# Eight of sixteen gate tiles as seven block products, with sums of the normed tokens kept in the residual's buffer

## Chip, cores and metric

One core of one Trainium2 chip runs the whole kernel in one launch. The metric is device time in microseconds (us), median of several runs. "Before" is the kernel as it stood, "after" the changed one.

## What is computed

One encoder layer on 1024 tokens of 1024 channels in float32. The part that matters here is the middle, where the normed tokens u meet one large input projection:

```python
u = rms_norm(h, mix_norm[i])
z = u @ w_in[i]
q, k, v, s_in, gates = jnp.split(z, splits, axis=-1)
y_attn = neighbourhood_attention(q..., k..., v..., na_rpb[i]) @ w_attn_out[i]
y_ssm = s5_branch(s_in, ...) @ w_ssm_out[i]
g_attn, g_ssm = jnp.split(jax.nn.sigmoid(gates), N_BRANCH, axis=-1)
h = h + (g_attn * y_attn + g_ssm * y_ssm) @ w_out[i]
```

In front of it and behind it stands a SwiGLU feed-forward block; a per-layer embedding and a last norm end the kernel. `gates` has 2048 columns: 16 tiles of 128 columns.

## The kernel before, in words

Everything lies transposed: channels on the 128 partitions, tokens along the free dimension, in two halves t = 0 and 1 of 512 tokens. A product in float32 accuracy is made by `mm3` of three matmuls on rounded parts (hi and lo of weight and tokens): hi times hi, hi times lo, lo times hi. `split` makes these parts: ScalarE casts hi, VectorE subtracts to get lo. One output tile of 128 columns for one half of the tokens (`proj`) takes 8 blocks of 128 channels, so 24 matmuls of 512 tokens.

The feed-forward blocks already run their large products in seven block products instead of eight (a 2 by 2 block scheme of the Strassen-Winograd kind). The names are in `A7` (which token operand: a block of the tokens, or one of the sums s1 to s4), `ACC7` (which of three PSUM banks X, Y, Z it adds to) and `NEW7`; `b_operand` makes the weight operand of product i from four raw weight blocks, in place, and splits it.

The middle part runs in this order on TensorE, and that order is the one in which the code is written. First `sin`, the four tiles of the state-space input, in two groups of two tiles, with two gate tiles (`gate_tile`, tile name gt) between; then `v`; then four rounds over head pairs (hp), each with the pair's q and k tiles (`qk_proj`) and 2, 2, 2 and 6 gate tiles; then the rest. A generator, `mixer_side`, is stepped by `tick()` once after every `mm3`. It sets between these matmuls, one after the other:

- the norm of the second token half (`u_second`), which writes the normed tokens to a scratch tile xn and splits them into u;
- 16 `inject` steps (8 small matmuls each: the state-space input of two groups, read back from memory, tile names ut and fmi) that fill the state buffer X, which uses the bytes of the residual's buffer h;
- the scan over X on GpSimd (`scan_steps`, 128 steps of three operations, each step needing the one before);
- 64 units of attention (8 heads, 2 row blocks, 4 column blocks). Unit j does the scores s of j, the transposes pt of unit j-3 and the products O of unit j-5. Between, VectorE adds the bias and takes the row maximum (sm), ScalarE takes the exponential, VectorE the reciprocal, ScalarE scales; pt is copied and split by ScalarE (pth) and VectorE (ptl). From unit 48 on each unit also starts one of 16 `ssm_out` steps: xs is copied out of X when the scan has ended, operands emi are loaded, and the products yo follow three units later;
- the state-space branch's gated linear unit (glu).

`yield n` in that generator means: go on after n ticks. A unit takes 4 ticks (12 large matmuls), and 3 from unit 48 on. A unit whose head pair has not been projected yet waits for it in the written order (`while hd not in qkv: yield 1`).

VectorE, ScalarE, GpSimd and the DMA queue of SyncE (SP) each have an order of their own here, made ahead of time by a planner that places an instruction when it expects its inputs and its buffer; at run time every engine and queue keeps that order and waits where it must. Buffers come from pools: 56 of 2 KB for each partition (tag x; u alone holds 32), 12 of 4 KB (tag w: split weights, q, k, xs), 3 of 4 KB (st: raw weights) and 4 (tmp).

Of the kernel before, what the change touches and what calls it, by code (L numbers as in the profile page):

```python
# [8 lines left out]
F32 = mybir.dt.float32  # L9
# [29 lines left out]
def encoder_block(ctx, tc, I, out):  # L39
# [22 lines left out]
    def tx(name, dt=F32R):  # L62
        return tl("x", NX, [P, HT], dt, name)
# [20 lines left out]
    def tmq(name, shape=(P, HT)):  # L84
        return at("tmp", shape, F32, name)
# [100 lines left out]
    def hsl(t):  # L186
        return slice(t * HT, (t + 1) * HT)
# [20 lines left out]
    class Norm:  # L208
# [37 lines left out]
            rstd(m, r, q)  # L246
            self.r = r

        def apply(self, gi, res, every):

            for j in range(NK):
                xn = tmq("xn")
                with behind_():
                    V.scalar_tensor_tensor(xn, self.h[j][self.t], gains[:, gi, j:j + 1], self.r, ALU.mult, ALU.mult)
                hi, lo = tx("xh"), tx("xl")
                split(hi, lo, xn)
                res.append((hi, lo))
                yield every
# [16 lines left out]
                    post(m)  # L275
            m0 += lead

    def halves(h, gi, store=None):


        xn = [[], []]
        nn = [Norm(h, 0), Norm(h, 1)]

        def done(m, t):
            nn[t].add(m)
            if store is not None:
                store(m, t)

        def first():
            yield 22  # L290
            nn[0].stat()
            yield 4
            yield from nn[0].apply(gi, xn[0], 5)

        def second(wait, every):
            yield wait
            nn[1].stat()
            yield every
            yield from nn[1].apply(gi, xn[1], every)

        return xn, done, first, second

# [17 lines left out]
    class Seven:  # L320
# [71 lines left out]
        def put(self, name, src):  # L392
            hi, lo = self.a21[len(self.ops[name])] if name == "a21" else (tx("xh"), tx("xl"))
            if self.plain:
                split(hi, lo, src)
                self.ops[name].append((hi, lo))
                return
            with behind_():
                self.last.append(split(hi, lo, src).ins)
            self.ops[name].append((hi, lo))  # L400
# [18 lines left out]
                    self.put(name, self.h[j0 + k][1])  # L419
                    yield 1  # L420

    def b_operand(blk, i):

        b11, b12, b21, b22 = blk
        if i in (2, 3, 6):
            V.tensor_tensor(b11, (b12, b22, None, None, b21)[i - 2], b11, ALU.subtract)  # L426
        elif i == 5:
            V.tensor_tensor(b12, b22, b12, ALU.subtract)
        hi, lo = tw("wh", [P, HT]), tw("wl", [P, HT])
        mark["ins"] = split(hi, lo, (b21, b11, b11, b11, b22, b12, b11)[i]).ins  # L430
        return hi, lo

# [563 lines left out]
    def store_h(m, t):  # L996
        nc.scalar.dma_start(h_d[:, (2 * m + t) * HT:(2 * m + t + 1) * HT], h[m][t])

    u, done, u_first, u_second = halves(h, 1, store_h)

    def t0_done():
        start(u_first())
# [36 lines left out]
    def proj(w, t, name):  # L1039
        o = bank(name)  # L1040
        for k in range(NK):
            mm3(o, w[k], u[t][k], k == 0, k == NK - 1)
            tick()
        return o


    X = tl("h", 1, [P, 2 * XR], F32, "X")
    Xt = X[:, 0:1]
# [4 lines left out]

    Xv = X.rearrange("p (r g n) -> p r g n", r=2, g=NPAIR)

    def load_u(pr):
        ut = thid("ut", [P, 2, NCH], F32)
        nc.sync.dma_start(ut, u_d[2 * pr:2 * pr + 2].rearrange("g p c -> p g c"))
        return ut

    def inject_load(pr):
        fm = thid("fmi", [P, HT], F32)
        nc.sync.dma_start(fm, f_d[pr])
        return load_u(pr), fm

    def inject(pr, ut, fm):
        o = bank("inj")
# [218 lines left out]
    stored = set()  # L1286

    def mixer_side():
        yield from u_second(14, 1)
        yield 8  # L1290
        for r in range(2):
            V.memset(Xv[:, r, :, 0:1], 0.0)
            V.memset(Xv[:, r, :, XP - 1:XP], 0.0)
        ld = {}
        for pr in range(NPAIR):
            if pr in (0, 8):
                while pr // 4 not in stored:
                    yield 1
                yield 8
                ld[pr] = inject_load(pr)  # L1300
                yield 8
# [67 lines left out]
    for m0 in range(0, 4, 2):  # L1369
        W = [(loadw if m0 else lambda src: loadh(src, "hid", "hid"))(win[12 + m0 + i]) for i in range(2)]  # L1370
        Wx = [loadw(win[16]), loadw(win[17])] if m0 == 0 else []
        su = [tst("su"), tst("su")]
        for t in range(2):
            for i in range(2):
                o = proj(W[i], t, "sin")
                A.copy(su[i].rearrange("p (s c) -> p c s", s=L)[:, t * 64:(t + 1) * 64, :],
                       o.rearrange("p (c s) -> p c s", s=L))
            for i, w in enumerate(Wx):
                gate_tile(w, i, t)
        for i in range(2):  # L1380
            for g in range(8):
                nc.sync.dma_start(u_d[8 * (m0 + i) + g].rearrange("(s i) c -> i s c", s=L),
                                  su[i][g * 16:(g + 1) * 16].rearrange("i (s c) -> i s c", s=L))
            stored.add(m0 + i)


    Wv = [loadw2(I["wv"][i]) for i in range(4)]
# [46 lines left out]
            res += [(hi[:, ksl(k)], lo[:, ksl(k)]) for k in range(4)]  # L1434
        return res

    gm = 2
    for hp in range(4):
        wq, wk = loadw(win[hp]), loadw(win[4 + hp])
        w = loadw(win[16 + gm])  # L1440
        qk_proj(hp, wq, wk)
        n = 2 if hp < 3 else 6
        for i in range(n):
            wn = loadw(win[17 + gm]) if i < n - 1 else None
            for t in range(2):
                gate_tile(w, gm, t)
            gm += 1
            w = wn
# [313 lines left out]
```

## Time and profile before

| what | us |
|---|---|
| runs | 2116.14, 2117.87, 2118.72; median 2117.87 |
| the profiled execution's own time | 2118.57 |
| its span, first to last instruction | 2116.8 |
| TensorE busy | 2089.2 (99%) |
| VectorE, ScalarE, GpSimd busy | 1416.2, 978.3, 387.3 |
| first `sin` matmul, first attention unit, last unit's scores | 685.2, 836.8, 1086.3 |

The page of the profile gives busy time, the span in 40 slices, the chain of work that ended last and the costliest groups. Views of the trace used below: the timeline (start, duration, instruction, and in brackets the idle time before it with what ended it), groups by line, windows (busy time of each engine in a stretch), and waits. A matmul's duration in it overlaps the next one's; what counts on TensorE is the distance from start to start.

### The profile page before, as it was taken

How to read it: one execution, taken by the hardware profiler on the slowest of the kernel's cores; microseconds unless marked ns; L12 is line 12 of the kernel's file. 1: busy time of each engine (PE TensorE's matmuls, PEld its weight loads, DVE VectorE, ACT ScalarE, POOL GpSimd, SP SyncE). 2: the span in 40 equal slices, each digit the busy share in tenths (PEclk: the TensorE clock that was granted, in tenths of full speed). 3: DMA queues.
4: the chain of work that ended last, by engine and by line, in shares of the span. 5: the costliest groups of instructions: out<-in, count | busy, mean ns of one | idle time of the engine just before them, and what ended most of it. 6: DMA issues, size and time to landing. Idle time of an engine off the chain costs nothing.

```text
span 2116.8 us, 28037 instructions
## 1 busy us (share of the span) xinstructions
PE 2089.2 (99%) x9708; PEld 1716.0 (81%) x9708; DVE 1416.2 (67%) x2416; ACT 978.3 (46%) x1793; POOL 387.3 (18%) x620
## 2 busy tenths in 40 slices
PE   8999999999999999999999999999999999999998
PEld 3788888888888888888888788788888888888886
DVE  7897776667967334777743666896565665785855
ACT  6434333334445344666764422553333334445544
POOL 0047555540000007888100000000000000000000
PEclk9999999999999999999999999999999999999999
DMA  3435444485543552223577631242423338533302
GB/s 132 142 117 153 128 130 131 138 282 157 183 120 106 157 179 67 82 82 96 150 200 260 209 105 52 93 155 95 129 80 120 100 100 290 171 107 95 116 24 80
DMA packets 195150, 280.98 MB, mean 133 GB/s; under 512 B 41280, under 2 KB 80320, under 8 KB 195008
## 3 DMA queue, kind: packets, MB, share of 16 engines
q1 hardware_dynamic: 180160, 258.22, 38.9%
q10 hardware_dynamic: 14848, 20.98, 2.9%
q8 instruction: 76, 1.25, 0.2%
q14 instruction: 66, 0.54, 0.1%
HBM read 196.81 MB, written 82.31 MB: 132 GB/s over the span
## 4 chain that ended last, share of the span: by engine, by line
PE 90%; DVE 5%; ACT 2%; DMA 1%; issue 1%; SPq 0%; DVEq 0%; ACTq 0%
PE dx L182 4%; PE dx L183 4%; PE dx L184 4%; PE ux L182 3%; PE gx L182 3%; PE ux L183 3%; PE ux L184 3%; PE gx L184 3%; PE gx L183 3%; PE gt L182 3%; PE gt L183 3%; PE gt L184 3%; PE dy L183 2%; PE dy L182 2%; PE dy L184 2%; PE uy L182 2%
## 5 line engine op out<-in xcount | busy, mean ns | idle before, releaser
L151 ACT CAST wh<-hbuf 128x512 fp32r<-128x512 f32 x280 | 172.9, 622 | 391.9 <-PE gx L183 81.9
L152 DVE TENSOR_TENSOR wl<-hbuf,wh 128x512 fp32r<-128x512 f32 x280 | 210.5, 754 | 124.3 <-ACT wh L151 122.0
L151 ACT CAST wh<-wblk 128x512 fp32r<-128x512 f32 x162 | 100.5, 623 | 166.9 <-PE dx L183 72.7
L152 DVE TENSOR_TENSOR wl<-wblk,wh 128x512 fp32r<-128x512 f32 x162 | 111.8, 692 | 46.6 <-ACT wh L151 41.2
L152 DVE TENSOR_TENSOR al<-araw,ah 128x512 fp32r<-128x512 f32 x154 | 106.4, 695 | 51.1 <-PE dx L183 21.1
L182 PE MATMUL dx<-ah,wh 128*128 128x512 f32 x352 | 137.9, 392 | 0.3 <-DVE hbuf L692 0.3
L1094 POOL TENSOR_TENSOR sc<-X,rho 128x128 f32<-128x128 f32 x128 | 78.1, 610 | 327.6 <-ACT X L1077 317.7
L184 PE MATMUL dx<-ah,wl 128*128 128x512 f32 x352 | 137.0, 389 | 0.0
L183 PE MATMUL dx<-al,wh 128*128 128x512 f32 x352 | 136.9, 389 | 0.0
L182 PE MATMUL gx<-xh,wh 128*128 128x512 f32 x320 | 124.9, 390 | 1.2 <-DVE c L579 1.2
L182 PE MATMUL ux<-xh,wh 128*128 128x512 f32 x320 | 125.1, 391 | 0.1
L184 PE MATMUL ux<-xh,wl 128*128 128x512 f32 x320 | 124.5, 389 | 0.0
L184 PE MATMUL gx<-xh,wl 128*128 128x512 f32 x320 | 124.5, 389 | 0.0
L183 PE MATMUL gx<-xl,wh 128*128 128x512 f32 x320 | 124.5, 389 | 0.0
L183 PE MATMUL ux<-xl,wh 128*128 128x512 f32 x320 | 124.5, 389 | 0.0
L151 ACT CAST ah<-araw 128x512 fp32r<-128x512 f32 x154 | 94.8, 619 | 45.6 <-PE dx L183 12.6
L182 PE MATMUL gt<-xh,wh 128*128 128x512 f32 x256 | 102.7, 401 | 0.0
L184 PE MATMUL gt<-xh,wl 128*128 128x512 f32 x256 | 99.8, 390 | 0.0
L183 PE MATMUL gt<-xl,wh 128*128 128x512 f32 x256 | 99.8, 390 | 0.0
L426 DVE TENSOR_TENSOR hbuf<-hbuf 128x512 f32<-128x512 f32 x120 | 91.3, 762 | 2.1
L182 PEld LDWEIGHTS dx<-ah,wh 128*128 128x128 f32 x352 | 66.1, 188 | 14.9 <-DVE hbuf L692 0.7
L183 PEld LDWEIGHTS dx<-al,wh 128*128 128x128 f32 x352 | 66.1, 188 | 13.9 <-issue 0.5
(376 smaller groups left out, 5719.8 us busy)
## 6 DMA issues: line engine op xcount, KB each, us to landing
araw<-a_d SPq DMA_DIRECT2D x154, 256.0 KB
a_d<-c SPq DMA_DIRECT2D x148, 256.0 KB
wblk<-in_wd SPq DMA_DIRECT2D x88, 256.0 KB
hbuf<-in_wg SPq DMA_DIRECT2D x40, 512.0 KB
hbuf<-in_wu SPq DMA_DIRECT2D x40, 512.0 KB
wst<-in_win SPq DMA_DIRECT2D x26, 512.0 KB
hbuf<-in_xT SPq DMA_DIRECT2D x32, 256.0 KB
h_d<-hbuf ACTq DMA_DIRECT2D x32, 256.0 KB
```

The source lines that it names most:

```text
L151: A.copy(hi, src)
L152: return eng.tensor_tensor(lo, src, hi.bitcast(F32), ALU.subtract)
L182: T.matmul(o, lhsT=wh, rhs=xh, start=first, stop=False, skip_group_check=more)
L183: T.matmul(o, lhsT=wh, rhs=xl, start=False, stop=False, skip_group_check=more)
L184: T.matmul(o, lhsT=wl, rhs=xh, start=False, stop=last, skip_group_check=more)
L426: V.tensor_tensor(b11, (b12, b22, None, None, b21)[i - 2], b11, ALU.subtract)
L1094: G.tensor_tensor(sc, both, rho4, ALU.mult)
```

## The change

Gate tiles 0 to 7 (of 16) are taken out of the places named above and computed in a stage of their own, between `sin` and `v`, in four groups of two tiles. Each group takes seven block products of 12 matmuls. For these, the token sums s1 to s4 are made by a new generator `u_sums`: the norm's `apply` with `keep` writes the normed tokens back into the residual's buffer h in place of xn, and the sums are made there, in place. The four `sin` tiles run first, all for t = 0 and then all for t = 1, with `u_second` and `u_sums` beside them. `mixer_side` starts only then; its inject steps now come every 6 ticks inside the gate stage, and their two loads share one buffer of the w pool (inj). The four rounds over head pairs keep 0, 1, 1 and 4 gate tiles; a unit of attention takes 2 or 3 ticks in turn, and 2 from unit 48 on.

```diff
-        def apply(self, gi, res, every):
+        def apply(self, gi, res, every, keep=False):
             for j in range(NK):
-                xn = tmq("xn")
+                xn = self.h[j][self.t] if keep else tmq("xn")
...
-    def b_operand(blk, i):
+    def b_operand(blk, i, packed=False):
...
-        hi, lo = tw("wh", [P, HT]), tw("wl", [P, HT])
+        if packed:
+            w = tw("wg")
+            hi, lo = w[:, 0:HT], w[:, HT:2 * HT]
+        else:
+            hi, lo = tw("wh", [P, HT]), tw("wl", [P, HT])
...
+    def u_sums(every):
+        a, b, c, d = ([h[j0 + k][t] for k in range(4)] for t in range(2) for j0 in (0, 4))
+        def put(name, src, lo=None):
+            hi, lo = tx("xh"), tx("xl") if lo is None else lo
+            split(hi, lo, src)
+            seven.setdefault(name, []).append((hi, lo))
+        for k in range(4):
+            V.tensor_tensor(d[k], c[k], d[k], ALU.add)
+            V.tensor_tensor(c[k], a[k], c[k], ALU.subtract)
+            put("s1", d[k])
+            yield every
+        for k in range(4):
+            V.tensor_tensor(a[k], d[k], a[k], ALU.subtract)
+            V.tensor_tensor(b[k], b[k], a[k], ALU.subtract)
+            put("s2", a[k])
+            yield every
+        while not sin_done:
+            yield 1
+        for name, src in (("s4", b), ("s3", c)):
+            for k in range(4):
+                if k % 2 == 0:
+                    two = tw("sl")
+                put(name, src[k], two[:, hsl(k % 2)])
+                yield every
+    seven = {"a12": u[0][4:], "a11": u[0][:4]}
+    start(chain(u_second(8, 1), u_sums(1)))
+    W = [loadh(win[12 + m], "hid", "hid") for m in range(2)] + [loadw(win[14 + m]) for m in range(2)]
+    su = [tw("su", dt=F32) for _ in range(4)]
...
+    for t in range(2):
+        for m in range(4):
+            o = proj(W[m], t, "sin")
+            A.copy(su[m]..., o...)
+            if t == 1:
+                for g in range(8):
+                    nc.sync.dma_start(u_d[8 * m + g]..., su[m][g * 16:(g + 1) * 16]...)
+            elif m > 1:
+                gate_raw(0, m - 2)
...
     def mixer_side():
-        yield from u_second(14, 1)
...
-            if pr in (0, 8):
-                while pr // 4 not in stored:
-                    yield 1
-                yield 8
-                ld[pr] = inject_load(pr)
-                yield 8
-            if pr % 8 < 7:
+            if pr == 0:
+                ld[0] = inject_load(0)
+                yield 4
+            if pr < NPAIR - 1:
                 ld[pr + 1] = inject_load(pr + 1)
             inject(pr, *ld.pop(pr))
-            yield 3
+            yield 6
...
-            yield 4 if j < SO else 3
+            yield 2 + (j % 2 if j < SO else 0)
...
+    def gate_seven(gp, i):
+        hi, lo = gops.pop((gp, i))
+        a, z = ACC7[i], gz.setdefault(gp, {})
+        if NEW7[i]:
+            z[a] = bank("g" + a.lower())
+        while len(seven.get(A7[i], ())) < 4:
+            force()
+        for k in range(4):
+            mm3(z[a], (hi[:, ksl(k)], lo[:, ksl(k)]), seven[A7[i]][k], NEW7[i] and k == 0, k == 3, not NEW7[i])
+            tick()
+        with tc.high_priority(offset=PRI):
+            c = (11, 11, 22, 12, 12, 22, 21)[i]
+            if i in (0, 2, 3, 6):
+                z[c] = tmp("gs")
+                A.copy(z[c], z[a])
+            else:
+                V.tensor_tensor(z[c], z[a], z[c], ALU.add)
+            if i in (1, 4, 5, 6):
+                gate_out(2 * gp + c % 10 - 1, c // 10 - 1, z[c])
...
+    for n, (gp, i) in enumerate(items):
+        if i in (0, 3):
+            gate_raw(gp + 1, i // 3)
+        gate_prep(*(items + [(4, 0)] * 3)[n + 3])
+        gate_seven(gp, i)
...
-    gm = 2
+    gm = 8
     for hp in range(4):
         wq, wk = loadw(win[hp]), loadw(win[4 + hp])
-        w = loadw(win[16 + gm])
+        n = (0, 1, 1, 4)[hp]
+        w = loadw(win[16 + gm]) if n else None
         qk_proj(hp, wq, wk)
-        n = 2 if hp < 3 else 6
```

TensorE has 9106 rows before and 9058 after. The first place to look at is the start of the gate work on TensorE. Before, a gate tile (gt) follows the second `sin` tile of the first half:

```order
L183 MATMUL sin_6207<-xl_6010,whh_6163 128x512
L184 MATMUL sin_6207<-xh_6009,whl_6164 128x512
L182 MATMUL gt_6253<-xh_5746,wh_6169 128x512
L183 MATMUL gt_6253<-xl_5747,wh_6169 128x512
L184 MATMUL gt_6253<-xh_5746,wl_6170 128x512
```

After, all `sin` tiles are done, the first product goes to bank Z (gz), the first inject step (inj) follows it, then the second product (bank X, gx):

```order
L183 MATMUL gz_6566<-xl_6002,wg_6550 128x512
L184 MATMUL gz_6566<-xh_6001,wg_6550 128x512
L1131 MATMUL inj_6582<-inj_6547 128x128 x4
L182 MATMUL gx_6596<-xh_5745,wg_6553 128x512
L183 MATMUL gx_6596<-xl_5746,wg_6553 128x512
```

So the first inject step stands 12 matmuls behind the last `sin` tile, and the next ones 18 matmuls apart. Their loads stand on the SP queue. Before, with the stores of the state-space input (u_d from su) in groups of 8 and the loads (fmi, ut) behind each:

```order
L1382 DMA u_d<-su 16x8x128 x8
L1058 DMA ut<-u_d 128x2x128
L1063 DMA fmi<-f_d 128x512
L1058 DMA ut<-u_d 128x2x128
L1382 DMA u_d<-su 16x8x128 x8
```

After, the load of the first step stands behind 16 of these stores, that of the second behind all 32:

```order
L1101 DMA u_d<-su 16x8x128 x16
L1123 DMA inj<-f_d 128x512
L1124 DMA inj<-u_d 128x2x128
L1101 DMA u_d<-su 16x8x128 x16
L1123 DMA inj<-f_d 128x512
L1124 DMA inj<-u_d 128x2x128
```

The second place is attention unit 48, the first that needs the last head pair. On TensorE before, its scores (s) stand 21 large matmuls behind the pair's last k matmul:

```order
L182 MATMUL gt<-xh,wh 128x512
L183 MATMUL gt<-xl,wh 128x512
L184 MATMUL gt<-xh,wl 128x512
L1209 MATMUL s<-kh,qs 128x288
L1210 MATMUL s<-kl,qs 128x288
```

After, three gate matmuls lie between the last k matmul and these scores:

```order
L183 MATMUL k<-xl,wh 128x512
L184 MATMUL k<-xh,wl 128x512
L182 MATMUL gt<-xh,wh 128x512
L183 MATMUL gt<-xl,wh 128x512
L184 MATMUL gt<-xh,wl 128x512
L1270 MATMUL s<-kh,qs 128x288
L1271 MATMUL s<-kl,qs 128x288
```

On VectorE, the rows between the maximum of unit 47 (sm) and that of unit 48 are, before:

```order
L1213 ISA sm,stat<-s,tb 128x288
L1213 ISA stat 128x1
L1113 COPY xs<-X 64x256 x4
L1229 TENSOR_TENSOR ptl<-pt,pth 96x384
L1195 TENSOR_TENSOR tb<-row,colm 128x12x24
L1160 SCALAR_TENSOR_TENSOR kl<-k,kh 64x512 x2
L1217 RECIPROCAL stat<-stat 128x1
```

and after, with a weight's split (wl), two pieces of the bias table (tb), three reciprocals and the copies xs ahead of the lo part kl of the keys:

```order
L1256 TENSOR_TENSOR tb<-row,colm 128x384
L1278 RECIPROCAL stat<-stat 128x1
L152 TENSOR_TENSOR wl<-wst,wh 128x1024
L1290 TENSOR_TENSOR ptl<-pt,pth 96x384
L1256 TENSOR_TENSOR tb<-row,colm 128x12x24
L1278 RECIPROCAL stat<-stat 128x1
L1174 COPY xs<-X 64x256 x2
L1278 RECIPROCAL stat<-stat 128x1
L1174 COPY xs<-X 64x256 x2
L1221 SCALAR_TENSOR_TENSOR kl<-k,kh 64x512 x2
```

The feed-forward blocks ahead of and behind the middle part keep their order, except that the first half's norm and splits, near the end of the first block, stand a few rows elsewhere on ScalarE and VectorE.

More of the change, by code (lines that the diff above doesn't have):

```diff
@@ L276, in down, with halves @@
             m0 += lead
-    def halves(h, gi, store=None):
+    def halves(h, gi, store=None, keep=False):
         xn = [[], []]
@@ L292, in first @@
             yield 4
-            yield from nn[0].apply(gi, xn[0], 5)
+            yield from nn[0].apply(gi, xn[0], 5, keep)
         def second(wait, every):
@@ L298, in second @@
             yield every
-            yield from nn[1].apply(gi, xn[1], every)
+            yield from nn[1].apply(gi, xn[1], every, keep)
         return xn, done, first, second
@@ L997, in store_h @@
         nc.scalar.dma_start(h_d[:, (2 * m + t) * HT:(2 * m + t + 1) * HT], h[m][t])
-    u, done, u_first, u_second = halves(h, 1, store_h)
+    u, done, u_first, u_second = halves(h, 1, store_h, True)
     def t0_done():
@@ L1044, in proj, with gate_raw @@
         return o
+    def u_sums(every):
[26 more added lines that the diff above has]
+    su = [tw("su", dt=F32) for _ in range(4)]
+    sin_done = []
+    gbl = {}
+    def gate_raw(gp, i):
+        if gp < 4:
+            st = tst("graw")
+            nc.sync.dma_start(st, win[16 + 2 * gp + i])
+            b = gbl.setdefault(gp, [None] * 4)
+            b[i], b[2 + i] = st[:, 0:HT], st[:, HT:2 * HT]
+    for t in range(2):
+        for m in range(4):
+            o = proj(W[m], t, "sin")
+            A.copy(su[m].rearrange("p (s c) -> p c s", s=L)[:, t * 64:(t + 1) * 64, :],
+                   o.rearrange("p (c s) -> p c s", s=L))
+            if t == 1:
+                for g in range(8):
+                    nc.sync.dma_start(u_d[8 * m + g].rearrange("(s i) c -> i s c", s=L),
+                                      su[m][g * 16:(g + 1) * 16].rearrange("i (s c) -> i s c", s=L))
+            elif m > 1:
+                gate_raw(0, m - 2)
+    seven["a22"] = u[1][4:]
+    sin_done.append(True)
+    drain()
     X = tl("h", 1, [P, 2 * XR], F32, "X")
@@ L1054, in encoder_block, with inject_load @@
     Xv = X.rearrange("p (r g n) -> p r g n", r=2, g=NPAIR)
-    def load_u(pr):
-        ut = thid("ut", [P, 2, NCH], F32)
+    def inject_load(pr):
+        both = tw("inj", dt=F32)
+        ut = both[:, HT:HT + 2 * NCH].rearrange("p (g c) -> p g c", g=2)
+        nc.sync.dma_start(both[:, 0:HT], f_d[pr])
         nc.sync.dma_start(ut, u_d[2 * pr:2 * pr + 2].rearrange("g p c -> p g c"))
[L1059 to L1064, printed above, removed]
+        return ut, both[:, 0:HT]
     def inject(pr, ut, fm):
@@ L1284, in glu_out @@
         nc.scalar.dma_start(y2_d[ksl(m), hsl(t)], sg)
-    stored = set()
     def mixer_side():
-        yield from u_second(14, 1)
-        yield 8
         for r in range(2):
@@ L1366, in gate_tile, with gate_prep, gate_out @@
         nc.sync.dma_start(g_d[m, :, hsl(t)], gs)
[L1369 to L1384, printed above, removed]
+    gops, gz = {}, {}
+    def gate_prep(gp, i):
+        if gp < 4:
+            gops[gp, i] = b_operand(gbl[gp], i, True)
+    def gate_out(m, t, z):
+        nc.sync.dma_start(g_d[m, :, hsl(t)], z)
+    def gate_seven(gp, i):
[17 more added lines that the diff above has]
+                gate_out(2 * gp + c % 10 - 1, c // 10 - 1, z[c])
+    items = [(gp, i) for gp in range(4) for i in range(7)]
+    for it in items[:3]:
+        gate_prep(*it)
+    for n, (gp, i) in enumerate(items):
[3 more added lines that the diff above has]
+        gate_seven(gp, i)
     Wv = [loadw2(I["wv"][i]) for i in range(4)]
```

1 line of the change is left out of this document (removed).

## The prediction

> **What bounds the kernel now.** First the page: busy time, GpSimd's line of the 40 slices, and the chain that ended last.
>
> ```profile
> PE 2089.2 (99%) x9708; PEld 1716.0 (81%) x9708; DVE 1416.2 (67%) x2416; ACT 978.3 (46%) x1793; POOL 387.3 (18%) x620
> POOL 0047555540000007888100000000000000000000
> PE 90%; DVE 5%; ACT 2%; DMA 1%; issue 1%; SPq 0%; DVEq 0%; ACTq 0%
> ```
>
> TensorE is the bound almost everywhere, so the next views are the waits of TensorE and the windows of the middle part: attention units 0 to 47, then unit 48 up to the first glu matmul.
>
> ```profile
> PE yo L1119 <- DVE ot L1244: 1.8, 1, 1.8
> PE v L1395 <- DVE wl L152: 0.6, 1, 0.6
> PE dn L182 <- ACT mh L151: 1.4, 1, 1.4
> ```
>
> ```profile
> 836.80:1019.80 183.00, 183.00 (x1066) 158.88 (x1065) 132.49 (x314) 127.28 (x282) 150.38 (x316) 1.00 0.28 82
> 1019.80:1125.30 105.50, 103.69 (x669) 92.16 (x669) 55.13 (x143) 72.74 (x162) 0.00 (x0) 1.00 0.71 203
> ```
>
> The columns of a window are PE, PEld, DVE, ACT, POOL, then granted clock, DMA share, GB/s. In 183 us of attention TensorE never waits. From 685 to 1195 us only two waits are told, 1.8 and 0.6 us. So matmuls taken out here shorten the kernel one for one, as long as what TensorE now covers still fits under it. The other engines are not idle, though: VectorE is busy for 72% and ScalarE for 70% of the first window.
>
> **What goes.** A gate tile takes 24 matmuls for each token half. Eight tiles take 8 x 2 x 24 = 384; four groups of seven products of 12 take 336. That is 48 fewer, as the listings of both kernels show (9106 rows, 9058). That the change doesn't remove them is thereby excluded. The price of 48 stands in the timeline as one run of exactly 48:
>
> ```profile
> 696.92 0.40 PE L182 MATMUL gt<-xh,wh 128*128 128x512 f32 x1
> ...
> 707.82 0.39 PE L182 MATMUL sin<-xh,whh 128*128 128x512 f32 x1
> ```
>
> 707.82 - 696.92 = **10.90 us**, 0.227 us each. The two waits above (2.4 us together) stand in places that the change rewrites; I take them out too and count what new waits come in.
>
> **The start of the gate stage.** VectorE must finish the second half's norm and splits, then the sums, then the first weight operand, before TensorE is done with `sin`.
>
> ```profile
> L182 PE MATMUL sin<-xh,whh x32: 389/389/791, 685.2 to 718.0; 128*128 128x512 f32 x32
> ```
>
> These are the first two `sin` tiles, by tile; the start is 685.2. The norm's rows, from the timeline:
>
> ```profile
> 694.68 1.02 PE L241 MATMUL ms<-acc,ones 128*128 128x512 f32 x2
> 697.97 0.69 DVE L206 SCALAR_TENSOR_TENSOR rs<-rq,rs 128x512 f32<-128x512 f32 x1
> 698.70 2.74 DVE L254 SCALAR_TENSOR_TENSOR xn<-hbuf,gains,rs 128x512 f32<-128x512 f32 x4
> 702.49 2.49 DVE L152 TENSOR_TENSOR xl<-xn,xh 128x512 fp32r<-128x512 f32 x4
> ```
>
> From ms to the first xn it is 4.0 us. After, ms stands 24 matmuls behind the start at 685.2, at 690.7; with a second weight split between, I put xn at 696. Behind it stand 8 xn (0.685 each by the row of four), 16 adds (taken as xn), 24 splits (0.62 each) and the first weight operand: 16.4 + 14.9 + 0.6 = 32 us, so 728. `sin` ends 192 matmuls and one ms after 685.2, at 729.6. u of the second half is ready at 696 + 5.5 + 5.0 = 706.5, needed from 707.8. Both are covered, by a little over 1 us: nothing in the sum, up to 3 us in the range.
>
> **The second inject step** stands 12 + 18 matmuls and one inject (8 small matmuls, an estimate of half a large one each, 0.9 us) behind 729.6, at 737.5. Its loads wait in the SP queue behind the stores of all four `sin` tiles.
>
> ```profile
> 718.90 1.08 ACT L1376 COPY su<-sin 128x512 f32<-128x512 f32 x1 [4.36 <-PE sin L184]
> 720.00 3.85 SPq L1382 DMA_DIRECT2D u_d<-su x8
> 685.35 0.80 SPq L159 DMA_DIRECT2D wst<-in_win x2
> 689.39 1.05 ACT L151 CAST wh<-wst 128x1024 fp32r<-128x1024 f32 x1 [2.62 <-DMA wst<-in_win]
> 1026.33 2.45 DMA vf<-v_d
> ```
>
> The last tile's copy (1.08 us, 1.1 to the first store) is done by 730.8; its eight stores take 3.9, the two loads 1.0 (at 0.48 an issue, like the stores). They are issued by 735.7. A landing takes between 2.45 us (the small vf) and 4.0 (512 KB of wst, from 685.35 to 689.39). So 738 to 739.6, 0.5 to 2.1 us late: **+1.0**. Later steps have their loads queued 10 us ahead. The weights of `v`, whose buffers come free only in the last products, get **+0.5** (0 to 1.2: nothing, or twice the 0.6 of before).
>
> **Units 0 to 47.** All 64 units by tile, what a unit itself costs TensorE, and how much time its operands have to spare:
>
> ```profile
> L1209 PE MATMUL s<-kh,qs x64: 292/317/340, 836.8 to 1086.3; 128*128 128x288 f32 x32, 128*128 128x384 f32 x32
> ```
>
> ```profile
> 1038.53 0.34 PE L1209 MATMUL s<-kh,qs 128*128 128x384 f32 x1
> 1039.62 0.22 PE L1239 MATMUL O<-ptl,vhl 96*64 96x128 f32 x1
> ```
>
> and in another unit:
>
> ```profile
> 958.04 0.54 DVE L1229 TENSOR_TENSOR ptl<-pt,pth 96x384 fp32r<-96x384 f32 x1
> 962.10 0.30 PE L1237 MATMUL O<-pth,vhl 96*128 96x128 f32 x1
> ```
>
> From s to the last O it is 1.15 us. With 12 large matmuls that makes 3.87, with 6 or 9 in turn 2.51 and 3.19, so 2.85 us a unit. The second pair of rows belongs to unit 28, one of the tightest: ptl is ready 3.5 us before O needs it, two units later. Two units will be 2.0 us shorter, so 1.5 us remain. VectorE's 132.5 us of busy work in these units becomes some 8 less, since gate weights leave, in 48 x 2.85 = 137 us: 91%. That is tight but not over, and back-to-back operations overlap (four splits in 2.49 us where one takes 0.68). I take **+1.0**; the ends are 0 and 17 us, the latter if no unit can go below the 3.2 us that 9 matmuls give (0.35 x 48). None of the units can gain: TensorE has no wait there to lose.
>
> **Unit 48.** Its scores come three matmuls behind the last k matmul of the last head pair, but need k cast, scaled and split first.
>
> ```profile
> L1160 DVE SCALAR_TENSOR_TENSOR kl<-k,kh 64x512 fp32r<-64x512 f32 x27 | 18.6, 688 | 1.8 <-ACT kh L1158 1.3
> L1157 ACT ACTIVATE kh<-k 64x512 fp32r<-64x512 f32 x13 | 7.7, 594 | 5.3 <-DVE kl L1160 4.8
> ```
>
> From the end of k: kh 0.6, two kl 1.4, so 2.0 us, against 0.5 us of matmuls: 1.4 us of waiting if both engines are free. On VectorE a weight split and copies of X stand ahead; that adds half a microsecond to 2.5. **+2.0** (1.4 to 4).
>
> **Unit 48 to glu.** Here the trace has little to spare already:
>
> ```profile
> 1049.54 0.56 DVE L1229 TENSOR_TENSOR ptl<-pt,pth 128x384 fp32r<-128x384 f32 x1 [0.46 <-ACT pth L1228]
> 1050.27 0.31 PE L1237 MATMUL O<-pth,vhl 128*128 128x128 f32 x1
> ```
>
> In unit 50, O starts 0.17 us behind its ptl. Each of the 16 units loses 3 matmuls, 0.68 us, of cover; the loads of emi, the copies of X and the softmax stay. If nothing of it is limited, 0; if these units keep their length, 16 x 0.68 = 10.9 us. Most are not as tight as unit 50: **+3.0**.
>
> **glu.** The last gelu's split and the glu:
>
> ```profile
> 1123.64 0.68 DVE L152 TENSOR_TENSOR yl<-yg,yh 128x512 fp32r<-128x512 f32 x1
> 1125.34 0.39 PE L182 MATMUL glu<-yh,wgh 128*128 128x512 f32 x1
> ```
>
> This is the fourth operand (of k = 3), needed 9 matmuls into glu, at 1127.4: 3.1 us to spare. Behind the last yo stand 87 large matmuls where 99 stood, 2.7 us less. **+0.5** (0 to 2.7).
>
> **The sum.** 2118.57 (span 2116.8 and 1.8 around it) - 10.9 - 2.4 + 1.0 + 0.5 + 1.0 + 2.0 + 3.0 + 0.5 = 2113.3. The profiled execution lies 0.7 above the median of the runs, so for the median: **2112.6**, 0.25% less.
>
> [...] The half clock: two stretches near the same place, one with the 1.4 us wait of dn, one with the 1.8 us wait of yo:
>
> ```profile
> 1205.00:1223.00 18.00, 16.36 (x65) 12.81 (x64) 13.99 (x23) 5.63 (x10) 0.00 (x0) 0.91 0.28 90
> 1036.00:1054.00 18.00, 16.19 (x110) 14.53 (x109) 11.63 (x33) 11.06 (x28) 0.00 (x0) 1.00 0.71 210
> ```
>
> The first fell to a granted clock of 0.91 (1.6 us lost of 18), the second kept 1.00. So a wait at unit 48 may cost up to 1.6 us more; that is in the range. [...]
>
> GpSimd's scan slows where VectorE works. Its three operations by line, first in 800 to 830 us:
>
> ```profile
> L1094 POOL TENSOR_TENSOR sc<-X,rho 128x128 f32<-128x128 f32 x20 | 10.7, 534 | 319.2 <-ACT X L1077 317.7
> L1095 POOL TENSOR_TENSOR sc<-sc 128x64 f32<-128x64 f32 x20 | 7.9, 397 | 1.6
> L1096 POOL TENSOR_TENSOR X<-sc,X 128x64 f32<-128x64 f32 x19 | 7.1, 372 | 1.5
> ```
>
> and in 836 to 1107, the attention:
>
> ```profile
> L1094 POOL TENSOR_TENSOR sc<-X,rho 128x128 f32<-128x128 f32 x106 | 65.4, 617 | 8.3
> L1096 POOL TENSOR_TENSOR X<-sc,X 128x64 f32<-128x64 f32 x106 | 44.9, 423 | 8.3
> L1095 POOL TENSOR_TENSOR sc<-sc 128x64 f32<-128x64 f32 x106 | 41.3, 390 | 8.3
> ```
>
> Busy and idle together, a step takes 1.5 us there and 1.66 here. After, the scan starts at about 812 (the last inject: 737.5 and 15 times 4.97). TensorE then needs the rest of the gates, `v` (192 matmuls) and q and k (96), to about 890: some 52 steps, and 76 in attention: it ends near 1016, and the copies xs, queued ahead of kh and of softmax scaling, come at about 1030. [...]
>
> **The rivals.**
> - *All is covered.* For it: no wait in 183 us. Then only the 1.4 us of unit 48 remain: 2117.9 - 13.3 + 1.4 = 2106. Against it: unit 50. Chance 0.15.
> - *The last 16 units keep their length*, since ptl, the loads and the SP queue set it. 2112.6 + 8 = 2120.5. For it: 0.17 us in unit 50. Against: most units had more. 0.20.
> - *The softmax engines become the bound of units 0 to 47* (slower). VectorE's 91% with waits for ScalarE in between stretch a unit from 2.85 to 3.2 us: 2112.6 + 16 = 2128.5. It decides from 2.98 on, where the forecast gain of 5.3 us is gone (0.11 x 48). For it: 72% in 3.81 us a unit. Against: 1.5 us to spare at unit 28. 0.10.
> - *The scan is late*: from 1.85 us a step in attention (76 steps, 14 us more), xs holds up softmax; at 2.0, about 10 us: 2122.6. 0.05.
> - *The forecast*, 2109 to 2116: 0.50.
>
> **Numbers.** A measurement of this kernel tells 0.2% (4.2 us) from no change, so faster means below 2113.6, slower above 2122.1. Faster: 0.15 and 0.36 of the forecast's 0.50. Same: 0.14 and most of the second rival. Slower: the third and the scan, and a little of the second. 0.51, 0.31, 0.18. The range leaves out the slower rivals and the best end: 2107 to 2121.5.
>
> **What would show it.** In the trace after: 48 fewer matmuls of 0.227 us; TensorE's waits by line: inj (1 us), s of unit 48 for kl (2), O or yo in the last units (3 together), glu (0.5); the distance of s from s near 2.85 us in units 6 to 47; xs starting without a wait for GpSimd. Wrong would be: s to s at 3.0 or more there, waits for the gate operands (wg) or for inj in each step, or a `v` that waits several microseconds.

## The result and the profile after

The changed kernel takes 2138.45 us (median of 5 runs, 2135.92 to 2142.33) against 2117.87 (5 runs, 2116.14 to 2120.48): 1.0100 times the time before, 95% interval 1.0086 to 1.0114. That is 20.6 us slower. The prediction was 2112.6, faster, with a range up to 2121.5. It was wrong in sign and in range.

The page of the changed kernel, in the lines that were shown of before (busy time, GpSimd in 40 slices, the chain that ended last):

```profile
PE 2090.6 (98%) x9660; PEld 1713.3 (80%) x9660; DVE 1457.8 (68%) x2496; ACT 995.5 (47%) x1831; POOL 390.1 (18%) x620
POOL 0047464640000006888200000000000000000000
PE 87%; DVE 7%; ACT 3%; DMA 2%; issue 1%; SPq 1%; ACTq 0%; DVEq 0%
```

TensorE has 48 matmuls fewer, and yet is busy 1.4 us longer; the chain runs over VectorE and ScalarE for 10% in place of 7%. The waits of TensorE between 600 and 1400 us say on what (engine, tile, line, releaser; us in total, times, longest). Rows that stand in both kernels are left out:

```profile
PE O L1298 <- ACT pth L1289: 6.1, 3, 2.8
PE gx L182 <- DVE gs L1448: 4.2, 4, 1.7
...
PE pt L1286 <- ACT sm L1279: 2.4, 1, 2.4
...
PE s L1271 <- DVE kl L1221: 1.9, 1, 1.9
PE s L1270 <- ACT kh L1219: 1.9, 1, 1.9
PE inj L1131 <- DMA inj<-u_d: 1.4, 1, 1.4
...
PE O L1300 <- DVE ptl L1290: 1.3, 4, 0.5
PE yo L1180 <- ACT vhl L1233: 0.9, 1, 0.9
PE q L184 <- DVE wl L152: 0.7, 1, 0.7
```

Together 20.8 us, where before there were 2.4. In four places behind these waits TensorE also ran at half its clock (granted clock 0.50 in windows of one microsecond, 990 to 993 for one). The windows around them (columns as in the prediction; the seventh is the granted clock):

```profile
987.00:996.00 9.00, 6.55 (x34) 5.56 (x33) 6.62 (x20) 6.12 (x16) 7.92 (x14) 0.81 0.53 169
1044.00:1050.00 6.00, 6.00 (x32) 5.22 (x32) 3.90 (x10) 4.05 (x10) 0.00 (x0) 0.72 0.12 30
1071.00:1080.00 9.00, 7.73 (x37) 7.01 (x38) 5.90 (x18) 7.72 (x19) 0.00 (x0) 0.62 0.78 241
1128.00:1134.00 6.00, 5.51 (x21) 4.46 (x21) 3.15 (x6) 4.32 (x8) 0.00 (x0) 0.72 0.71 209
```

9 x 0.19 + 6 x 0.28 + 9 x 0.38 + 6 x 0.28 = 8.5 us of clock, part of it in time in which TensorE waited anyway. The account: from the first `sin` matmul to the first matmul of the output projection (dn) it was 512.2 us (685.2 to 1197.4) and is 532.2 (684.8 to 1217.0), so all 20 us are here. -10.9 for the matmuls, -2.4 for the old waits, +20.8 and +8.5 make +16; the other 4 these views do not tell. Gaps too small for the view of waits are likely, and not shown.

By stage, from the starts of the first matmuls; the lower rows are kernels of the next section:

| us | first sin to unit 0 | units 0 to 47 | unit 48 to glu | glu to dn |
|---|---|---|---|---|
| before | 151.6 | 183.0 | 105.5 | 72.1 |
| changed | 213.2 | 143.5 | 106.2 | 69.3 |
| changed, with cover put back | 212.9 | 183.0 | 107.8 | 72.1 |
| changed, tile behind the last pair | 213.2 | 139.1 | 97.1 | 70.7 |
| four tiles, early scan | 167.5 | 166.7 | 104.9 | 66.7 |
| six tiles, early scan | 187.1 | 140.4 | 107.3 | 72.1 |

The windows of the two attention stages, to be set beside those of before:

```profile
898.00:1041.50 143.50, 138.45 (x856) 120.78 (x854) 119.19 (x307) 113.97 (x266) 113.17 (x229) 0.99 0.28 78
1041.50:1147.70 106.20, 96.36 (x603) 85.04 (x604) 56.42 (x145) 75.19 (x163) 0.00 (x0) 0.94 0.67 196
```

The second row is the heart of it: 603 matmuls take 106.2 us where 669 took 105.5, although 66 matmuls of 0.227 us, 15.0 us, are gone. Most units did get shorter: of the fifteen distances from one unit's scores to the next's, eleven are 0.6 to 0.7 us shorter than before, as three matmuls less should make them, and one is 2.7 shorter (its old wait is gone). Three are longer, and so is the way from the last unit's scores to glu (40.6 us against 39.0, with 21 matmuls fewer). The longest of the three starts at unit 55; here are its scores and the next unit's, before and then after:

```profile
1049.76 0.29 PE L1209 MATMUL s<-kh,qs 128*128 128x288 f32 x1
1054.36 0.29 PE L1209 MATMUL s<-kh,qs 128*128 128x288 f32 x1
1068.57 0.29 PE L1270 MATMUL s<-kh,qs 128*128 128x288 f32 x1
1078.73 0.30 PE L1270 MATMUL s<-kh,qs 128*128 128x288 f32 x1
```

10.16 us in place of 4.60. What TensorE waits for in it is the product O of unit 50, five units back, whose operand pth comes late from ScalarE:

```profile
1069.02 1.65 ACT L1174 COPY xs<-X 64x256 f32<-64x256 f32 x4
1070.68 1.04 ACT L151 CAST wh<-wst 128x1024 fp32r<-128x1024 f32 x1
1071.63 0.47 ACT L1289 CAST pth<-pt 128x384 fp32r<-128x384 f32 x1
1072.15 0.47 PE L1298 MATMUL O<-pth,vhl 128*128 128x128 f32 x1 [2.83 <-ACT pth L1289]
```

Four copies of X and a weight's cast run ahead of pth; the wait takes 2.8 us, and the clock behind it (the third of the windows above, 0.62) some 3.4.

What a wait looks like, in the timeline at unit 48 (start, duration, then what it waited for):

```profile
1038.95 0.39 ACT L1174 COPY xs<-X 64x256 f32<-64x256 f32 x1
1039.24 0.62 ACT L1279 ACTIVATE sm<-sm,stat 128x384 f32<-128x384 f32 x1
1039.87 0.40 ACT L1174 COPY xs<-X 64x256 f32<-64x256 f32 x1
...
1040.28 0.59 ACT L1218 ACTIVATE kh<-k 64x512 fp32r<-64x512 f32 x1
...
1041.53 0.40 PE L1270 MATMUL s<-kh,qs 128*128 128x288 f32 x1 [1.86 <-ACT kh L1219]
...
1042.40 1.38 DVE L1221 SCALAR_TENSOR_TENSOR kl<-k,kh 64x512 fp32r<-64x512 f32 x2
...
1043.83 0.41 PE L1271 MATMUL s<-kl,qs 128*128 128x288 f32 x1 [1.91 <-DVE kl L1221]
```

The keys' casts stand behind two copies of X and a softmax scaling on ScalarE, and their lo parts behind that; TensorE, three matmuls behind k, waits 3.8 us. No engine is slow here: kh takes 0.59 us and kl 0.69 in the mean, as before the change. Several things that had 21 matmuls of time now have three.

### The profile page after: what moved, and what is told of

Same layout as the page of the kernel before. It is cut to its first block, busy times and chain, and to the rows that moved or that the text cites. A ratio compares the mean times of both kernels' runs of the same rounds, so it can differ in the third digit from the quotient of the medians.

```text
span 2136.7 us, 28150 instructions
## 1 busy us (share of the span) xinstructions
PE 2090.6 (98%) x9660; PEld 1713.3 (80%) x9660; DVE 1457.8 (68%) x2496; ACT 995.5 (47%) x1831; POOL 390.1 (18%) x620
## 4 chain that ended last, share of the span: by engine, by line
PE 87%; DVE 7%; ACT 3%; DMA 2%; issue 1%; SPq 1%; ACTq 0%; DVEq 0%
PE gx L182 4%; PE gx L183 4%; PE gx L184 4%; PE dx L182 4%; PE dx L183 4%; PE dx L184 4%; PE ux L182 3%; PE ux L183 3%; PE ux L184 3%; PE gy L182 2%; PE gy L184 2%; PE gy L183 2%; PE dy L184 2%; PE dy L182 2%; PE dy L183 2%; PE uy L182 2%
## 5 line engine op out<-in xcount | busy, mean ns | idle before, releaser
L151 ACT CAST wh<-wblk 128x512 fp32r<-128x512 f32 x162 | 100.6, 623 | 165.9 <-PE dx L183 70.7
L184 PEld LDWEIGHTS dx<-ah,wl 128*128 128x128 f32 x352 | 66.1, 188 | 13.9
L182 PEld LDWEIGHTS gx<-xh,wh 128*128 128x128 f32 x320 | 60.1, 188 | 14.7 <-issue 2.2
L182 PEld LDWEIGHTS ux<-xh,wh 128*128 128x128 f32 x320 | 60.0, 188 | 13.1 <-issue 0.6
```

What stands on the lines that cost most here:

```text
L151: A.copy(hi, src)
L182: T.matmul(o, lhsT=wh, rhs=xh, start=first, stop=False, skip_group_check=more)
L184: T.matmul(o, lhsT=wl, rhs=xh, start=False, stop=last, skip_group_check=more)
```

## The experiments

The kernel before took 2117.20 us in the round of one to four, 2117.42 in that of five to eight and 2116.16 in that of nine to twelve. The runs of the changed kernel spread over 6 us, so differences from it of 3 us or less are not clear. The first four experiments ask where the loss sits. **One: bank X.** Product 6 of each group is done behind product 0 of the next.

```diff
-    items = [(gp, i) for gp in range(4) for i in range(7)]
+    items = [(0, 0)]
+    for gp in range(4):
+        items += [(gp, i) for i in range(1, 6)] + [(gp + 1, 0)] * (gp < 3) + [(gp, 6)]
```

> Product 6 of a gate group is done behind product 0 of the next group. Theory: product 6 adds to bank X, which product 5 has just left and VectorE still has to read, and nothing is computed between; so the four waits of gx for gs (4.2 us by line) shrink to the one of the last group, where 6 still follows 5 (about 1.8): 2138.5 - 3 = 2135.5. Rival: VectorE is simply late there with the copies of X and the weight differences, so that another product waits instead: 2138.5, within 1.

Measured: 2132.47 us, 6.0 less than the changed kernel, twice the 3 expected. One wait of gx is left, 1.7 us, at the last group, as expected; the wait for inj also fell, from 1.4 to 0.4. The way from the first sin to unit 0 fell from 213.2 to 209.0 us; why the rest of the kernel gave some 2 us too is open. In the changed kernel such a place reads, in the timeline:

```profile
820.47 2.91 DVE L152 TENSOR_TENSOR wl<-wst,wh 128x1024 fp32r<-128x1024 f32 x2
821.90 0.39 PE L184 MATMUL gx<-xh,wg 128*128 128x512 f32 x1
823.30 0.68 DVE L1448 TENSOR_TENSOR gs<-gx,gs 128x512 f32<-128x512 f32 x1
824.03 0.50 PE L182 MATMUL gx<-xh,wg 128*128 128x512 f32 x1 [1.75 <-DVE gs L1448]
```

The matmul at 821.90 is the last of product 5 and the next is the first of product 6, both in X; VectorE must read X in between. This is the longest of the four waits, and about 1 us of it is VectorE still at two weight splits (wl). The shortest, 0.34 us, has eight inject matmuls between the two products.

**Two: the block products themselves.** Same stage, plain tiles.

```diff
-    start(chain(u_second(8, 1), u_sums(1)))
+    start(u_second(8, 1))
...
-    items = [(gp, i) for gp in range(4) for i in range(7)]
...
+    wn = loadw(win[16])
+    for m in range(8):
+        w, wn = wn, loadw(win[17 + m]) if m < 7 else None
+        for t in range(2):
+            gate_tile(w, m, t)
```

> The same eight gate tiles in the same stage, but as plain tiles of 24 matmuls for each half; no sums, no block products; attention as in the changed kernel. Theory (the loss lies in the attention, which lost its cover, whatever the stage computes): + 10.9 for 48 matmuls, - 4.6 for the waits on bank X: 2144.8, with about 17 us of waits from unit 0 to glu as after. Rival (the block products, their sums in h and their buffers disturb what follows): attention runs as before, 2124 or less.

Measured: 2138.20 us, no more than with block products. The place is that of the theory: attention takes 144.1 and 103.9 us (143.5 and 106.2 in the changed kernel), with the same waits. The number is not. First sin to unit 0 takes 217.1 us against 213.2, so the block products bring 3.9 there where 6.3 was expected (in the order of experiment six, 207.9 us, they bring 9.2); and the two profiles differ by 3.3 us behind dn (916.4 and 919.7 us to the end), where nothing was changed.

**Three: the gelus.**

```diff
-        A.activation(sm, sm, AF.Exp, ...)
+        mark["exp"] = A.activation(sm, sm, AF.Exp, ...).ins
...
-        A.activation(yg, yt, AF.Gelu_apprx_tanh)
+        with tc.issue_after(mark["exp"]):
+            A.activation(yg, yt, AF.Gelu_apprx_tanh)
```

> The gelus of the state-space branch are queued on ScalarE behind the last exponential; nothing else. Theory: the gelu among the exponentials (two table loads of 1.28 and 1.06 of its own) is what holds pth up at 1110 (2.5 us of waiting), with what follows at 1126 (1.7) and half a clock afterwards: 2138.5 - 4.5 = 2134. Rival: glu then waits for the gelus instead: 2138.5, within 1.5.

Measured: 2135.70 us (2132.87 to 2137.44), 2.7 less, which is not clear of the spread, and not the 4.5 expected. In the trace the wait of O for pth at 1110 is gone, but O then waits 1.8 us for ptl in its place. So the two table loads among the exponentials (1.28 us each) are at most a small part of the loss.

**Four: cover put back.** Six tiles are computed a second time and not stored.

```diff
-            yield 2 + (j % 2 if j < SO else 0)
+            yield 4 if j < SO else 3
...
-    gm = 8
+    gm = 2
...
-        n = (0, 1, 1, 4)[hp]
+        n = 2 if hp < 3 else 6
...
-                gate_tile(w, gm, t)
+                if gm >= 8:
+                    gate_tile(w, gm, t)
+                else:
+                    A.copy(tmp("gs"), proj(w, t, "gt"))
```

> The gate stage as in the changed kernel, and behind it the attention of the kernel before: units of 4 and 3 ticks, 2, 2, 2 and 6 gate tiles, six of which are computed a second time and not stored. 288 matmuls more, 65.4 us. Theory (cover): the waits and half-clock stretches from unit 0 to glu, about 23.5 us, go down to the 2 us of before: 2138.5 + 65.4 - 21.5 = 2182. Rival (they come from what the gate stage leaves behind: late scan, late loads, buffers): they stay, 2204.

Measured: 2179.31 us; less the 65.4 of the 288 added matmuls, 2113.9. The waits of TensorE in that kernel, 600 to 1270 us:

```profile
PE gx L182 <- DVE gs L1448: 4.2, 4, 1.7
PE inj L1131 <- DMA inj<-u_d: 2.1, 1, 2.1
PE yo L1180 <- DVE ot L1305: 1.7, 1, 1.7
PE yo L1180 <- DMA emi<-u_d: 0.8, 1, 0.8
```

All waits of s, pt and O are gone and units 0 to 47 take 183.0 us, as before the change; unit 48 to glu keeps 2.3 us more than before. So the loss in attention goes when the cover is back. This run alone leaves open that something comes late from the gate stage, since the added matmuls also give it 65 us more time; experiment two (no block products, the same loss) and experiment twelve (an earlier scan, the same waits) speak against that. The gate stage taken alone gains about 2117.2 (before, in this round) - 2113.9 = 3.3 us, after paying for bank X and inj.

The next four undo single losses. **Five: one tile moved behind the last head pair.**

```diff
-        n = (0, 1, 1, 4)[hp]
+        n = (0, 1, 0, 5)[hp]
```

> The gate tile between the third and the last head pair goes behind the last pair (0, 1, 0, 5 tiles in place of 0, 1, 1, 4), so that 45 large matmuls in place of 3 stand between the last k matmul and unit 48. Theory (unit 48 comes too close behind k): its waits for kh and kl (3.8 us) and the half clock behind them (1.7) go: 2138.5 - 5 = 2133.5. Rival (ScalarE and VectorE are behind at this place for other reasons: copies of X, weight splits): the wait turns up a unit later, 2137 or more.

Measured: 2125.55 us, 12.9 less, far more than unit 48's own 5. Its waits for kh and kl are gone, as the theory says. From unit 48 to glu it now takes 97.1 us in place of 106.2, with the same 603 matmuls: the long step from unit 55 to 56 takes 4.5 us in place of 10.2, and its wait for pth is gone. Units 0 to 47 take 139.1 in place of 143.5: the wait at unit 32 fell from 2.4 to 0 and a new one of q for a weight split, 1.9 us, came at unit 29. So the place of one tile changes which operands come late all along; how it reaches unit 55 is not shown.

**Six: the order of products** 1, 0, 3, 2, 5, 4, 6, so that the first output block is written from X and Z is added to it, not the other way round.

```diff
-            if i in (0, 2, 3, 6):
+            if i in (1, 2, 3, 6):
                 z[c] = tmp("gs")
                 A.copy(z[c], z[a])
...
-            if i in (1, 4, 5, 6):
+            if i in (0, 4, 5, 6):
                 gate_out(2 * gp + c % 10 - 1, c // 10 - 1, z[c])
...
+    PREP, TURN = (1, 0, 2, 3, 5, 4, 6), (1, 0, 3, 2, 5, 4, 6)
...
```

> Products of every group in the order 1, 0, 3, 2, 5, 4, 6, so that no product adds to a bank that the one just ahead has left. Theory (bank X): all four waits of gx for gs go, also that of the last group which product 6 behind the next 0 kept: 2132.5 - 1.7 = 2130.8. Rival: VectorE is late and other products wait: 2132.5 or more.

Measured: 2129.74 us, 8.7 less than the changed kernel; no wait of gx is left, so the order of the products made these waits. From the first sin to unit 0 it takes 207.9 us in place of 213.2, somewhat more than the 4.2 us of waits.

**Seven and eight: fewer tiles by block products**, so that attention keeps more plain ones, both in the order of six.

```diff
-    gm = 8
+    gm = 4
...
-        n = (0, 1, 1, 4)[hp]
+        n = (1, 2, 1, 6)[hp]
...
-            yield 2 + (j % 2 if j < SO else 0)
+            yield 3 + j % 2 if j < SO else 3
```

> Only four gate tiles (two groups) by block products, in the order of the run before; twelve plain tiles, 1, 2, 1 and 6 behind the head pairs; units of 3 and 4 ticks in turn, 3 from unit 48 on. 24 matmuls less than before the change, 5.45 us. Theory (what counts is cover): attention runs as before, the gate stage waits for inj only (1.4): 2117.2 - 5.45 + 1.4 = 2113. Rival (half a tick less for each unit is already too little): several us of waits, 2117 or more.

Measured: 2117.44 us, ratio 1.0001 (0.9992 to 1.0010): no change, and not the theory's 2113. With six tiles the same lines read `gm = 6`, `(0, 1, 1, 6)` and `2 + (j % 3 > 0) if j < SO else 3`:

> Six gate tiles (three groups) by block products in that order; ten plain tiles, 0, 1, 1 and 6 behind the head pairs; units of 2, 3, 3 ticks in turn up to 47, 3 from unit 48 on, where as much cover stands as before the change. 36 matmuls less, 8.2 us. Theory (the loss lies in the last 16 units and in the third quarter): 2117.2 - 8.2 + 1.4 (inj) + 1 (q) + 1 = 2112.5. Rival (units of 2.67 ticks wait as in the third quarter of the changed kernel, 5 us and the half clock): 2117 or more.

Measured: 2123.97 us, ratio 1.0030 (1.0019 to 1.0041). Both rivals' numbers, but not for the rivals' reason. In the kernel with six tiles one wait is left that matters, here in the view of waits:

```profile
PE pt L1286 <- ACT sm L1279: 8.3, 1, 8.3
```

and in the timeline, on ScalarE and VectorE just ahead of its end:

```profile
1021.63 1.65 ACT L1174 COPY xs<-X 64x256 f32<-64x256 f32 x4 [7.49 <-POOL X L1157]
1021.63 1.20 DVE L1174 COPY xs<-X 64x256 f32<-64x256 f32 x3 [5.97 <-POOL X L1157]
```

The scan on GpSimd ends after unit 48 is due; the copies of X wait for it at the head of both queues, and the softmax stands behind them. With four tiles it is the same, with 6.17 us on ScalarE and 2.5 at pt. It is the prediction's rival "the scan is late", in kernels where the other waits no longer hide it.

**Nine to twelve: the scan earlier.** The same edit on four kernels:

```diff
             if pr == 0:
                 ld[0] = inject_load(0)
-                yield 4
+                yield 8
...
             inject(pr, *ld.pop(pr))
-            yield 6
+            yield 4
```

> The kernel with four tiles by block products, and the inject steps every 4 ticks in place of 6, the first of them 4 ticks later. Theory (there the scan on GpSimd ends after unit 48 is due, the copies xs wait for it for 6 us on ScalarE and VectorE with the softmax behind them): the scan starts some 20 us earlier, the wait of pt for sm (2.5 us), the half clock behind it (2.9) and most of the wait for inj (1.7) go: 2117.4 - 6 = 2111.5. Rival: something else holds the softmax at unit 48: 2117, within 1.5.

Measured: 2111.17 us (8 runs, 2107.94 to 2113.10), ratio 0.9974 (0.9964 to 0.9984). The wait is gone; what TensorE waits for between 600 and 1270 us is:

```profile
PE dn L182 <- ACT mh L151: 1.4, 1, 1.4
PE yo L1180 <- DMA emi<-u_d: 1.0, 2, 0.5
PE dn L183 <- DVE ml L152: 0.2, 1, 0.2
```

> The kernel with six tiles by block products, with the same two edits of the inject steps. Theory (scan): the 8.3 us wait of pt for sm at unit 48 and the half clock (1.8) go, and about 1 us at inj: 2124 - 11 = 2113. Rival: units of 2.67 ticks leave ScalarE and VectorE behind, the wait stays or spreads: 2119 or more.

Measured: 2110.80 us (8 runs, 2108.37 to 2114.37), ratio 0.9974 (0.9964 to 0.9985). Both beat the kernel before by 0.26%. Their windows of units 0 to 47 and of 48 to glu, first with six tiles:

```profile
871.80:1012.20 140.40, 140.04 (x874) 122.94 (x874) 118.36 (x305) 114.97 (x264) 118.92 (x240) 1.00 0.27 75
1012.20:1119.50 107.30, 103.91 (x669) 92.09 (x669) 56.75 (x148) 75.19 (x168) 0.00 (x0) 1.00 0.69 201
```

874 matmuls in 140.4 us, where the changed kernel took 143.5 for 856; and the granted clock is 1.00.

> All eight tiles by block products, with four edits together: the other order of the products, the gate tile behind the last head pair, the gelus behind the last exponential, the inject steps every 4 ticks. Theory (separate causes, so the gains add): 2138.5 - 8.7 - 12.9 - 2.7 - 1.4 = 2112.8, and lower if the scan holds something up. Rival (with 288 matmuls of cover less, one wait takes the place of another): 2119 or more.

Measured: 2122.65 us, ratio 1.0035 (1.0022 to 1.0047). The gains do not add: against the kernel before it is no better, clear of noise, than the moved tile alone (ratio 1.0039, 1.0025 to 1.0053). The gate stage does keep its part (206.6 us to unit 0, against 213.2), but unit 48 to glu goes from 97.1 to 101.5. In its timeline:

```profile
1057.61 2.48 ACT L1174 COPY xs<-X 64x256 f32<-64x256 f32 x6
1058.89 1.19 DVE L1174 COPY xs<-X 64x256 f32<-64x256 f32 x4
1060.12 0.56 DVE L1290 TENSOR_TENSOR ptl<-pt,pth 128x384 fp32r<-128x384 f32 x1
1060.73 0.27 PE L1300 MATMUL O<-ptl,vhl 128*64 128x128 f32 x1 [2.63 <-DVE ptl L1290]
```

Six copies on ScalarE and four on VectorE run ahead of the softmax and ptl in one lump, and O waits 2.6 us for ptl. That such lumps are all of the 4.4 us is not shown.

> The changed kernel with the edits of the inject steps alone. Theory: the scan is not what delays it, since the copies xs come 10 us behind the scan's end there; only the wait for inj goes: 2138.5 - 1.4 = 2137. Rival (the scan is late and delays unit 48): 2132 or less.

Measured: 2136.16 us (2133.84 to 2137.33), 2.3 less, within the spread and near the 2137 of the theory. The wait for inj is gone. The scan ends at 1007 us in place of 1029, and the waits of unit 48 for kh and kl stay (1.8 and 1.7 us). So in the changed kernel itself the scan is not the bound.

## Why the prediction was wrong, step by step

- **What goes, -10.9.** Right: the matmuls are gone, and they are worth it. From the first sin to unit 0, experiment six has 968 matmul rows and takes 207.9 us, experiment two 1016 rows and 217.1; with 1.3 us more of waits in six, the 48 are worth about 10.5.
- **Start of the gate stage, 0.** Right: no wait for the first weight operand, the sums or the second half.
- **Second inject, +1.0.** Right mechanism, 1.4 us. **v, +0.5:** no wait there; q waits for a weight split in its place, 0.7.
- **Left out of the sum: bank X.** The prediction counted products and operands, and asked of no product what had to leave its bank. Four waits, 4.2 us; experiment one removes three of them, experiment six all.
- **Units 0 to 47, +1.0.** For units 0 to 31 it held (88.8 us in all, one wait of 0.3). At unit 32 it did not: 2.4 us at pt and 1.7 of clock. The mean distance of s from s in units 6 to 47 is 3.09 us, beyond the 3.0 that the prediction named as a sign of being wrong. It comes from two places, at unit 32 (6.74 us) and in front of unit 48 (6.91); between them most distances alternate around 2.5 and 3.2, so the rival of a softmax that stretches every unit is not what happened. The step that failed took the mean load of VectorE (91%) and one operand's time to spare. The work comes in lumps at each head pair, as the timeline of the changed kernel shows on VectorE ahead of that wait:

```profile
984.63 1.40 DVE L1221 SCALAR_TENSOR_TENSOR kl<-k,kh 64x512 fp32r<-64x512 f32 x2
986.06 1.37 DVE L152 TENSOR_TENSOR wl<-wst,wh 128x1024 fp32r<-128x1024 f32 x1
987.46 0.55 DVE L1290 TENSOR_TENSOR ptl<-pt,pth 96x384 fp32r<-96x384 f32 x1
987.93 0.44 DVE L1274 CUSTOM_DVE_ANT_1 sm<-s,tb 128x288 f32<-128x288 f32 x1
```

  The softmax (sm) stands behind 2.8 us of keys and weights for the next pair, as long as a whole unit was reckoned to take (2.85).
- **Unit 48, +2.0 (1.4 to 4).** Right mechanism, at the upper end: 3.8, and 1.7 of clock, which the text had held possible.
- **Unit 48 to glu, +3.0 (0 to 10.9).** This is the step that failed and decided. Its waits are 6.1 + 0.8 + 0.9 = 7.8 us, and the clock lost in the last two windows 5.1: some 12.9, beyond the upper end. The window agrees: 105.5 less the old wait of 1.8 and the 15.0 of matmuls is 88.7 us, and the stage took 106.2; of these 17.5 more, 3.6 are unit 48's. The prediction spread a small loss over sixteen units, and its bound took for granted that a unit can at worst keep its old length. But most units gave up their 0.68 us as hoped, and a few got much longer than before: a late operand stops TensorE for up to 2.8 us, and behind some of these waits the granted clock falls to 0.50 too. The longest wait is that for the unit that the prediction called tight, O of unit 50. (The O shown there reads pth; the first O that reads ptl stands 0.32 us behind it.) "Most units had more" was true, and says nothing of the price of those that had not. The rival "the last 16 units keep their length" has the right total (105.5 and 106.2 us) by luck: eleven distances got shorter and three longer. **glu, +0.5:** no wait.
- **The half clock.** The prediction allowed 1.6 us for one drop; four came, together 8.5 us by the windows of the changed kernel, and no wait of TensorE ahead of them was longer than 2.8 us.
- **The scan.** As a rival wrong here, right in experiments seven and eight, where it was the wait that mattered (2.5 and 8.3 us at pt). The working had it end near 1016; it ended at 1029: a step took 1.61 us up to 898 and 1.72 from there on, where it reckoned with 1.5 and 1.66. VectorE was busy for 29% of the first stretch and 83% of the second (before, 33% of 800 to 830 and 72% of the attention), so the slower steps stand where VectorE is busier; that its work is what slows them is not shown. The copies xs came 10 us behind the scan's end, as expected without a wait for GpSimd.

What stays open: how the 20 us split exactly between waits, clock and small gaps, since each wait moves the next; why moving one tile also took away the wait for O of unit 50; and why the gains of the single edits don't add in the last 16 units beyond the copies that the trace shows.

## What to carry to other kernels

Work of the bound engine that hides another chain is not free to remove (here 48 matmuls less made 20.6 us more): before taking it out, look at what each of the covered engines does in its densest few microseconds there, not at its mean load. The saving should be taken where the cover is plenty (here the first units and the gate stage: six tiles, with the last 16 units left as they were and the scan started earlier, gave 0.26%), and a removed wait can uncover the next one (here 2.5 and 8.3 us behind the scan in experiments seven and eight), so look for the second in the queue. A product that adds to an accumulator which another engine has still to read wants a different product between (here four waits of gx, 4.2 us, and none in the order of experiment six).

## What was not expected of the hardware

TensorE's clock fell to half around waits of less than 3 us: windows of one microsecond of the changed kernel show 0.50 from 990 to 993, 1045 to 1047, 1072 to 1078 and 1130 to 1133. Three of these drops follow waits of 2.4, 1.9 + 1.9 and 2.8 us, the fourth two waits of only 0.8 and 0.5 us close together; the wait of 2.5 us at 1110 was followed by none (1.00 from 1109 to 1118). The waits for bank X of up to 1.75 us left the clock at 1.00, and the same 1.4 us wait of dn cost clock in the profile of before (0.91 over 18 us) and none in that of the changed kernel (1.00 from 1228 to 1240). What decides between these, no run here shows.
